# Four projections and half of the output product with 512 moving weight columns, and the retention's gate written in place

## The chip, the cores and the metric

The kernel runs on one core of a Trainium2 chip. A core has a matrix engine (TensorE, PE in the profile; its weight loads are a row of their own, PEld), VectorE (DVE), ScalarE (ACT), GpSimd (POOL) and SyncE (SP), which issues most of the DMAs that bring weights from HBM into SBUF. Each engine works off its own queue in order. The metric is the device time of one execution in microseconds; less is better.

## The reference, cut to what matters

The model is two transformer blocks on 256 tokens of width 1024, with 256 context tokens beside them. All of the change lies in the mixer and the merge of the first block.

```python
(gq, gk, gv, gg, glr_f, glr_b, rq, rk, rv, rg, m_gla, m_ret) = split_columns(h @ w_in)   # widths 512, 512, 1024, 1024, 16, 16, 512, 512, 1024, 1024, 1024, 1024
o_f, s_gf = gla_scan(gq, gk, gv, log_gate(glr_f, 0), states[0], False)
o_b, s_gb = gla_scan(flip(gq), flip(gk), flip(gv), flip(log_gate(glr_b, 1)), states[1], True)
o_gla = rmsnorm(o_f + flip(o_b), gla_norm) * jax.nn.silu(heads(gg, GLA_HEADS))
# rq and rk are turned by axial_rope for the latent tokens
r_f, s_rf = retention_scan(rq, rk, rv, lg_f, states[2], False)
r_b, s_rb = retention_scan(flip(rq), flip(rk), flip(rv), lg_b, states[3], True)
o_ret = head_groupnorm(r_f + flip(r_b)) * jax.nn.silu(heads(rg, RET_HEADS))
...
y = jax.nn.sigmoid(m_gla) * (o_gla @ w_branch_gla) + jax.nn.sigmoid(m_ret) * (o_ret @ w_branch_ret)
h_lat = h_lat + g1 * (y @ w_out)
```

gv, rv, gk and rk are needed for the latent and for the context tokens ("two streams"); gq, gg, rg and w_out for the latent tokens alone. A mixture of experts (MoE), a sparse attention block, a cross attention and an MLP follow.

## The kernel before, in words

**Precision.** Every product of activations and weights is made of three matmuls: activations and weights are each split into a high part in TensorE's reduced fp32 form and a remainder, and high×high, high×low and low×high are summed in PSUM. `split` (L285 to L287) does it for weights: a CAST on ACT makes `hi`, a TENSOR_TENSOR on DVE, or on POOL where the caller asks for it, makes `lo` = weight minus `hi`. A split covers 128x1024 numbers, half of a load of 1 MB. The pools of `hi` and `lo` have two buffers, the ring of loaded weights `wt` three; the rows of w_ada that DVE multiplies by the conditioning vector (L473) are loaded into the same ring.

**Projections.** `w_step` (L299 to L301) keeps the weights stationary and moves 256 tokens (tile `pw`); gq, gk, rq and rk use it. `x_step` (L312 to L314) keeps a tile of 128 tokens stationary and moves 256 weight columns (tile `px`). gv, rv, gg, rg and w_out use it in chunks of 256 columns, four for each matrix: 96 matmuls a chunk with two streams, 48 with one. A result of a chunk takes one PSUM bank (both token tiles beside each other). PSUM has six such banks, and two for transposes (`tp`).

**The stages around the change, in order of time.** `z` (the decay gate's products, to about 88 us); cumulative sums of the gate by DVE scans (L730: eight for the latent tokens, `sums(0)`, then eight for the context); gv and gq; the levels of GLA (`gla_levels`): for each of 16 level steps DVE makes four differences `E` (L782 to L785), ACT an exponential (L786), DVE a product with q and k (L787), and PE eight matmuls `lev` (L794); beside them run rk, rq (by `w_step`) and rv (by `x_step`), the retention's constants `crow` (L907, L908) and the rows of w_ada (L473 to L475). Then `gates("g")`: for each chunk of gg the ACT tanh and DVE product `sg` (L960, L961), the GLA output gated in place (`og`, L970) and `parts_chunk`, which transposes it (`tp`, L364) and splits it into `oTg` (L371). Beside it, pulled from a generator, runs `ret`: the rotation of rk and rq (`rot`, L857; DVE L858 to L861), the retention's scores (`rs`, L870) and its states and outputs (`or`, L887). `gates("r")` does the same for rg; the four results are copied by POOL into `srg` (L979), from which DVE gates the normed output `orr` (L987). After the merge with the two branch matrices comes w_out in four chunks: DVE multiplies by g1 (`otmp`, L1076) and adds to `h` (L1077), ACT sums squares (`junk`, L383), PE transposes `h` (`tp`, L1152), DVE and ACT scale it to `h2T` (L1154, L1156), and PE forms the router's logits (`rt`, L1163). The MoE's expert loads begin behind that.

**Order.** The program is written as generators that are pulled in a fixed order, and a layer of the kernel then orders the recorded instructions for each engine by dependences and costs. What stands in each engine's queue is therefore shown below from the built programs and not from the source.

In rv and rg, `lows=(PO, None)` gives the first half of every chunk's `lo` to POOL: eight instructions in all.

Of the kernel before, what the change touches and what calls it, by code (L numbers as in the profile page):

```python
# [14 lines left out]
ALU = mybir.AluOpType  # L15
# [15 lines left out]
def _chunks(w):  # L31

    k, n = w.shape
    return w.reshape(k // 128, 128, n // 256, 256).transpose(2, 1, 0, 3).reshape(n // 256, 128, -1)

# [65 lines left out]
def prepare(inp):  # L101
# [14 lines left out]
    out['w1'] = np.concatenate([_chunks(a) for a in (gk, gq, gv, rk, rq, rv, gg, rg, mg, mr)])  # L116
# [3 lines left out]
    out['w2'] = np.concatenate([_chunks(g[n][0]) for n in ('w_branch_gla', 'w_branch_ret', 'w_out')])  # L120
# [125 lines left out]
def pull(gen, n):  # L246
    for _ in range(n):
        if next(gen, 0) == 0:
            return


class Kern:
# [253 lines left out]
    def mixer(self, PA, PB, PC):  # L506
# [190 lines left out]
        def vproj(base, names, tags, done=None):  # L697
            a = tb([128, 2, D], tags[0], name=names[0])
            b = tb([128, 2, D], tags[1], name=names[1])
            st[names[0]], st[names[1]] = a, b  # L700
            for c in range(4):
                pc, pl = done if done and c == 0 else self.proj_x('w1', base + c, [SC, SL], lows=(None, None) if base == 4 else (PO, None))
                nc.scalar.copy(b[:, :, c * 256:(c + 1) * 256], pc.rearrange("p (t n) -> p t n", t=2))
                v.tensor_copy(a[:, :, c * 256:(c + 1) * 256], pl.rearrange("p (t n) -> p t n", t=2))
                yield
# [18 lines left out]
        pull(gv, 1)  # L724
# [224 lines left out]
        def gates(which, base, gain, hi, lo):  # L949
# [5 lines left out]
            for c in range(4):  # L955
# [11 lines left out]
        for c, sg, gn in gates("g", 16, None, hi, lo):  # L967
            cs = slice(c * 256, (c + 1) * 256)
            for i in range(2):
                v.scalar_tensor_tensor(og[:, i, cs], og[:, i, cs], st['rg'][:, 2 * c + i:2 * c + i + 1], sg[:, i], op0=ALU.mult, op1=ALU.mult)  # L970
            if c:
                self.parts_chunk(og, c - 1, gn, hi, lo)
        self.og_parts = (hi, lo)
        sgs = []
        srg = ta([128, 2, D], "B8", name="srg")
        for c, sg, _ in gates("r", 20, None, None, None):
            if c == 0:
                self.parts_chunk(og, 3, gn, hi, lo)
            nc.gpsimd.tensor_copy(srg[:, :, c * 256:(c + 1) * 256], sg)  # L979
# [40 lines left out]
    def merge(self, PB, PC):  # L1020
# [47 lines left out]
        for c in range(4):  # L1068
            po, = self.proj_x('w2', 8 + c, [(yh, yl)], wt=w2[c])
            last = self.last  # L1070
            if c < 2:
                w2.append(self.load_w('w2', 10 + c))
                more(2)
            cs = slice(c * 256, (c + 1) * 256)
            tmp = tb([128, 2, 256], "t3", name="otmp", bufs=1)
            v.tensor_tensor(tmp, po.rearrange("p (t n) -> p t n", t=2), g1[:, None, cs].to_broadcast([128, 2, 256]), op=ALU.mult)  # L1076
            v.tensor_tensor(h[:, :, cs], h[:, :, cs], tmp, op=ALU.add)  # L1077
            if c:
                turned(c - 1)
            if c > 1:  # L1080
                with self.tc.issue_after(last):
                    logits(c - 2)
# [1240 lines left out]
```

## Time and profile before

| | us |
|---|---|
| runs | 1072.5, 1072.56, 1068.6 (median 1072.5) |
| the profiled execution: its own time | 1070.49 |
| its span in the trace | 1068.7 |
| PE busy | 1012.1 (95%), 7182 matmuls |
| DVE busy | 641.9 (60%) |
| ACT busy | 449.1 (42%) |
| POOL busy | 74.8 (7%) |

The times of the parts come from the one profiled execution; 1.8 us of its 1070.49 lie outside the span. A busy PE is not PE at its peak, since matmuls overlap: what one costs in a stream is the distance from its start to the next one's start, which is shorter than its duration. Idle time of an engine is printed with the instruction that ended it.

### The profile page before, as it was taken

The page shows a single profiled execution, that of the slowest core. Times are in us where ns is not written, and L with a number is a line of the kernel's source. Part 1 is how long each engine was busy: PE and PEld are TensorE (multiplying, and loading weights), DVE is VectorE, ACT ScalarE, POOL GpSimd, SP SyncE. Part 2 cuts the span into 40 slices and gives each one's busy share as a digit, 9 for nine tenths or more (in the row PEclk, how much of TensorE's full clock was granted, in tenths as well). Part 3 has the DMA queues.
Part 4 walks back from the last instruction along what each step waited for, and adds up shares of the span by engine and source line. Part 5 has one row for each costly group of instructions (what it writes and reads, how often), then busy time and mean ns, then how long its engine had stood idle before and what let it go on. Part 6 is the DMA issues. An engine that isn't in the chain of part 4 may idle for free.

```text
span 1068.7 us, 17877 instructions
## 1 busy us (share of the span) xinstructions
PE 1012.1 (95%) x7182; PEld 819.1 (77%) x7182; DVE 641.9 (60%) x1195; ACT 449.1 (42%) x785; POOL 74.8 (7%) x69
## 2 busy tenths in 40 slices
PE   5999998999999999999999878898999999999998
PEld 3889998998989999944444412687756889999997
DVE  4467879896565465634424312789776647555554
ACT  4356444333334634422222101685465646444442
POOL 0200001200131000000000000122100000000000
PEclk9999999999999999999999999999989999999999
DMA  9822654773327887888999999943311425555552
GB/s 357 313 73 79 241 193 158 178 277 111 118 83 284 320 350 274 246 309 322 387 420 420 420 421 421 383 158 120 119 40 40 159 82 194 189 182 186 193 197 79
DMA packets 36197, 243.07 MB, mean 227 GB/s; under 512 B 4032, under 2 KB 4432, under 8 KB 8464
## 3 DMA queue, kind: packets, MB, share of 16 engines
q1 hardware_dynamic: 34800, 236.53, 59.2%
q0 software_dynamic: 1312, 5.37, 1.5%
q8 instruction: 57, 0.93, 0.3%
q14 instruction: 28, 0.23, 0.1%
HBM read 240.83 MB, written 1.06 MB: 226 GB/s over the span
## 4 chain that ended last, share of the span: by engine, by line
PE 33%; DMA 12%; DVE 5%; ACT 2%; POOL 1%; issue 1%; SPq 0%; DVEq 0%; POOLq 0%; ACTq 0%
DMA wt<-wgu_in 7%; DMA wt<-wdn_in 4%; PE pw L299 3%; PE pw L300 3%; PE pw L301 3%; PE gu L1484 3%; PE acc L2292 3%; PE acc L2291 3%; PE acc L2293 3%; PE dn L1515 2%; DVE lo L287 1%; PE sc L1534 1%; POOL rstd L355 1%; DMA nfin<-nfin_in 1%; PE pT L2087 1%
## 5 line engine op out<-in xcount | busy, mean ns | idle before, releaser
L287 DVE TENSOR_TENSOR lo<-wt,hi 128x1024 fp32r<-128x1024 f32 x171 | 209.8, 1229 | 123.6 <-ACT hi L285 123.3
L285 ACT CAST hi<-wt 128x1024 fp32r<-128x1024 f32 x180 | 188.1, 1047 | 197.9 <-PE pw L300 113.2
L1484 PE MATMUL gu<-wt,XT 128*32 128x512 f32 (+1 forms) x608 | 92.2, 607 | 9.0 <-DMA wt<-wgu_in 8.9
L301 PE MATMUL pw<-fh,lo 128*128 128x256 f32 x352 | 98.2, 280 | 2.1 <-DVE lo L287 2.1
L300 PE MATMUL pw<-fl,hi 128*128 128x256 f32 x352 | 98.8, 281 | 1.1 <-DVE fl L371 1.1
L299 PE MATMUL pw<-fh,hi 128*128 128x256 f32 x352 | 98.5, 280 | 0.0
L1484 PEld LDWEIGHTS gu<-wt,XT 128*32 128x32 f32 (+1 forms) x608 | 23.3, 115 | 63.0 <-issue 43.7
L313 PE MATMUL px<-lo,h0h 128*128 128x256 f32 x240 | 68.6, 286 | 2.1 <-DVE lo L287 1.5
L301 PE MATMUL pw<-h0h,lo 128*128 128x256 f32 x240 | 68.1, 284 | 2.2 <-DVE lo L287 2.2
L312 PE MATMUL px<-hi,h0h 128*128 128x256 f32 x240 | 68.9, 287 | 0.0
L301 PEld LDWEIGHTS pw<-fh,lo 128*128 128x128 f32 x352 | 66.9, 190 | 2.4 <-DVE lo L287 2.4
L299 PE MATMUL pw<-h0h,hi 128*128 128x256 f32 x240 | 68.5, 285 | 0.1
L300 PE MATMUL pw<-h0l,hi 128*128 128x256 f32 x240 | 67.9, 283 | 0.0
L314 PE MATMUL px<-hi,h0l 128*128 128x256 f32 x240 | 67.9, 283 | 0.0
L300 PEld LDWEIGHTS pw<-fl,hi 128*128 128x128 f32 x352 | 66.1, 188 | 2.0 <-DVE fl L371 1.5
L299 PEld LDWEIGHTS pw<-fh,hi 128*128 128x128 f32 x352 | 66.1, 188 | 0.6
L1515 PE MATMUL dn<-wt,hT 128*32 128x512 f32 (+1 forms) x320 | 55.8, 596 | 4.9 <-DMA wt<-wdn_in 3.4
L1492 DVE TENSOR_TENSOR hid<-hid,gu 128x256 f32<-128x256 f32 x12 | 5.1, 421 | 78.6 <-ACT hid L1491 78.6
L2292 PE MATMUL acc<-lo,rh 128*128 128x512 f32 x128 | 49.8, 389 | 0.0
L2291 PE MATMUL acc<-hi,rh 128*128 128x512 f32 x128 | 49.8, 389 | 0.0
L2293 PE MATMUL acc<-hi,rlo 128*128 128x512 f32 x128 | 49.8, 389 | 0.0
L313 PEld LDWEIGHTS px<-lo,h0h 128*128 128x128 f32 x240 | 46.0, 192 | 3.3 <-DVE lo L287 2.0
(643 smaller groups left out, 2518.9 us busy)
## 6 DMA issues: line engine op xcount, KB each, us to landing
wt<-wgu_in SPq DMA_DIRECT2D x60, 1024.0 KB, 16.6
wt<-w_in SPq DMA_DIRECT2D x48, 1024.0 KB, 5.0
wt<-wdn_in SPq DMA_DIRECT2D x31, 1024.0 KB, 19.4
wt<-wada_in SPq DMA_DIRECT2D x16, 1024.0 KB, 5.3
wt<-wfi_in SPq DMA_DIRECT2D x16, 1024.0 KB, 4.8
wt<-wfo_in SPq DMA_DIRECT2D x16, 1024.0 KB, 4.8
wada<-wada_in SPq DMA_DIRECT2D x8, 1024.0 KB, 9.8
wt<-wxkv_in SPq DMA_DIRECT2D x4, 1024.0 KB, 6.4
```

The costliest lines, as they stand in the source:

```text
L285: nc.scalar.copy(hi, src)
L287: self.low = (engine or nc.vector).tensor_tensor(lo, src, hi.bitcast(F32), op=ALU.subtract).ins
L299: nc.tensor.matmul(o, lhsT=hi[:, c], rhs=xh[:, x, :], start=k == 0 and b == 0, stop=False)
L300: nc.tensor.matmul(o, lhsT=hi[:, c], rhs=xl[:, x, :], start=False, stop=False)
L301: nc.tensor.matmul(o, lhsT=lo[:, c], rhs=xh[:, x, :], start=False, stop=k == 7 and b == 1)
L312: nc.tensor.matmul(o, lhsT=xh[:, k, s], rhs=hi[:, c], start=k == 0 and t == 0, stop=False)
L313: nc.tensor.matmul(o, lhsT=xh[:, k, s], rhs=lo[:, c], start=False, stop=False)
L1484: return lambda: nc.tensor.matmul(pg[a:a + n, :], lhsT=XT[:, k, c:c + n], rhs=w[:, kk * 512:(kk + 1) * 512], start=k == 0, stop=k == 7)
L1515: return lambda: nc.tensor.matmul(pd[nh][a:a + m, :], lhsT=hT[:, kk, a:a + m], rhs=w[:, kk * 1024 + nh * 512:kk * 1024 + (nh + 1) * 512], ...
L2291: nc.tensor.matmul(a, lhsT=rh[:, k, s], rhs=whi[:, w], start=c == 0 and k == 0, stop=False)
L2292: nc.tensor.matmul(a, lhsT=rh[:, k, s], rhs=wlo[:, w], start=False, stop=False)
L2293: nc.tensor.matmul(a, lhsT=rlo[:, k, s], rhs=whi[:, w], start=False, stop=last)
```

## The change

A new layout `_wide` puts 512 columns of eight k-tiles into two loads of 1 MB, each with four k-tiles; a new function `proj_xw` works on it: a split covers two k-tiles of 512 columns, and each matmul moves 512 columns into a PSUM bank for each token tile. It is used for the second half of gv, for all of rv, gg and rg, and for the first half of w_out: 1056 matmuls of 256 columns become 528 of 512. As many splits are made as before, of the same size. `proj_xw` has no choice of engine for `lo`: the eight on POOL are DVE's. A pair of chunks now has one point (half of the loads) at which other work is pulled in, and at its end two banks, one for each token tile, where two chunks had two ends. `gates` makes `sg` for each token tile (128x512), and for rg DVE writes it into `srg` directly, so that the four POOL copies go. gq's two chunks are moved ahead of the second half of gv. In the output product the first two chunks are one pair, and the transposes of both follow chunk 2.

```diff
+def _wide(w):
+    n = w.shape[1]
+    return w.reshape(2, 4, 128, n // 512, 512).transpose(3, 0, 2, 1, 4).reshape(n // 256, 128, -1)
...
+    def proj_xw(self, name, i, streams, outs, wts=None):
+        nc = self.nc
+        outs += [[self.bank("px") for _ in range(2)] for _ in streams]
+        for half in range(2):
+            wt = wts[half] if wts else self.load_w(name, i + half)
+            for q in range(2):
+                hi, lo = self.split(wt[:, q * 1024:(q + 1) * 1024])
+                for kk in range(2):
+                    k = 4 * half + 2 * q + kk
+                    c = slice(kk * 512, kk * 512 + 512)
+                    for (xh, xl), banks in zip(streams, outs):
+                        for t, o in enumerate(banks):
+                            s = slice(t * 128, t * 128 + 128)
+                            nc.tensor.matmul(o, lhsT=xh[:, k, s], rhs=hi[:, c], start=k == 0, stop=False)
+                            nc.tensor.matmul(o, lhsT=xh[:, k, s], rhs=lo[:, c], start=False, stop=False)
+                            self.last = nc.tensor.matmul(o, lhsT=xl[:, k, s], rhs=hi[:, c], start=False, stop=k == 7).ins
+            yield half
...
         pull(gv, 1)
+
+        def gq(c):
+            pl, = self.proj_w('w1', 2 + c, [SL])
+            return nc.scalar.mul(QK[:, 2 * c:2 * c + 2, 0, :], pl.rearrange("p (h t) -> p h t", h=2), 128.0 ** -0.5).ins
...
-        pull(gv, 1)
+        gq(0)
         for r in range(2):
             nc.scalar.activation(xx[r][:, :, 1:257], xx[r][:, :, 1:257], AF.Ln, bias=one)
...
+        late = gq(1)
         sums(0)
-        for c in range(2):
-            pl, = self.proj_w('w1', 2 + c, [SL])
-            late = nc.scalar.mul(QK[:, 2 * c:2 * c + 2, 0, :], pl.rearrange("p (h t) -> p h t", h=2), 128.0 ** -0.5).ins
...
-            for c in range(4):
-                pl, = self.proj_x('w1', base + c, [SL], lows=(None, None) if which == 'g' else (PO, None))
-                pv = pl.rearrange("p (t n) -> p t n", t=2)
-                pull(bg, 2 if which == "g" else 3)
-                sg = tb([128, 2, 256], "t2", name="sg", bufs=2)
-                nc.scalar.activation(sg, pv, AF.Tanh, scale=0.5)
-                v.scalar_tensor_tensor(sg, sg, 1.0, pv, op0=ALU.add, op1=ALU.mult)
-                yield c, sg, gn
+            for c in (0, 2):
+                outs = []
+                for half in self.proj_xw('w1', base + c, [SL], outs):
+                    for f in between if c + half == 0 else ():
+                        f()
+                    pull(bg, 2 if which == "g" else 3)
+                for t, pv in enumerate(outs[0]):
+                    sg = tb([128, 512], "t2", name="sg", bufs=2)
+                    nc.scalar.activation(sg, pv, AF.Tanh, scale=0.5)
+                    to = sg if into is None else into[:, t, c * 256:c * 256 + 512]
+                    v.scalar_tensor_tensor(to, sg, 1.0, pv, op0=ALU.add, op1=ALU.mult)
+                    yield c, t, sg, gn
...
-            nc.gpsimd.tensor_copy(srg[:, :, c * 256:(c + 1) * 256], sg)
...
+        for half in self.proj_xw('w2', 8, [(yh, yl)], pair, wts=w2):
+            w2.append(self.load_w('w2', 10 + half))
+            more(2)
+        for t in range(2):
+            added(pair[0][t], t, slice(0, 512))
+        for c in range(2, 4):
             po, = self.proj_x('w2', 8 + c, [(yh, yl)], wt=w2[c])
...
+            if c == 2:
+                turned(0)
+            turned(c - 1)
+            with self.tc.issue_after(last):
+                logits(c - 2)
```

The order in the queues changes at three places. DVE, from the latent tokens' scans to the context's, before (E are a level's differences and products, `lo` a weight remainder, `gvl` a copy of a finished gv chunk):

```order
L730 SCALAR_TENSOR_TENSOR xcl<-mn,xcl 128x256 x3
L782 TENSOR_TENSOR E<-xcl 128x2x128
...
L287 TENSOR_TENSOR lo<-wt,hi 128x1024
L784 TENSOR_TENSOR E<-xcl 128x2x2x64
L785 TENSOR_TENSOR E<-xcl 128x2x2x64
L730 SCALAR_TENSOR_TENSOR xcc<-mn,xcc 128x256 x8
L742 TENSOR_SCALAR sfb<-xcc 128x4
L704 COPY gvl<-px 128x2x256
L287 TENSOR_TENSOR lo<-wt,hi 128x1024 x3
L787 TENSOR_TENSOR E<-E,QK 128x1024 x2
```

and after the change:

```order
L295 TENSOR_TENSOR lo<-wt,hi 128x1024
L827 TENSOR_TENSOR E<-E,QK 128x1024
L824 TENSOR_TENSOR E<-xcl 128x2x2x64
L295 TENSOR_TENSOR lo<-wt,hi 128x1024
L825 TENSOR_TENSOR E<-xcl 128x2x2x64
L773 SCALAR_TENSOR_TENSOR xcc<-mn,xcc 128x256 x4
L827 TENSOR_TENSOR E<-E,QK 128x1024
L773 SCALAR_TENSOR_TENSOR xcc<-mn,xcc 128x256 x4
L947 TENSOR_SCALAR ctr<-ctr 128x512 x2
L948 TENSOR_TENSOR crow<-ctr,crow 128x512 x2
L295 TENSOR_TENSOR lo<-wt,hi 128x1024
```

The last `lo` here is that of the second quarter of gv's wide pair. The context's scans, one product E and the four `crow` instructions stand between it and the `lo` before it; the `crow` instructions stood behind two more groups of `lo` before.

PE, from the rotation of rq to the retention's first scores, before (`tp` transposes a gated chunk, `px` is the projection of gg):

```order
L857 MATMUL rot<-rQ,rc 128x512 x2
L364 MATMUL tp<-smalls,og 128x128 x4
L313 MATMUL px<-lo,h0h 128x256
L314 MATMUL px<-hi,h0l 128x256
...
L870 MATMUL rs<-rQ,rK 128x256 x4
L312 MATMUL px<-hi,h0h 128x256
L870 MATMUL rs<-rQ,rK 128x256 x4
```

and after the change:

```order
L897 MATMUL rot<-rQ,rc 128x512 x2
L392 MATMUL tp<-smalls,og 128x128
L910 MATMUL rs<-rQ,rK 128x256 x4
L373 MATMUL px<-hi,h0h 128x512
```

The 23 `px` matmuls that stood between the transposes and the scores stand behind the scores now. DVE's queue at the same place, after the change:

```order
L1005 SCALAR_TENSOR_TENSOR sg<-sg,px 128x512 x2
L898 TENSOR_TENSOR rt<-rot,rc 128x512 x2
L900 TENSOR_TENSOR rQ<-rQ,rc 128x1024
L1014 SCALAR_TENSOR_TENSOR og<-og,rstd,sg 128x256
L901 TENSOR_TENSOR rQ<-rQ,rt 128x1024
L1014 SCALAR_TENSOR_TENSOR og<-og,rstd,sg 128x256 x3
```

Both products `sg` of the finished gg pair stand ahead of the rotation's four instructions; `og` of the lone transpose stands between its last two.

PE, at the end of chunk 2 of w_out, before:

```order
L314 MATMUL px<-hi,yl 128x256
L1152 MATMUL tp<-smalls,h 128x128 x4
L1163 MATMUL rt<-mconst,h2T 128x36 x4
L312 MATMUL px<-hi,yh 128x256
L1152 MATMUL tp<-smalls,h 128x128 x4
L313 MATMUL px<-lo,yh 128x256
```

and after the change:

```order
L322 MATMUL px<-hi,yl 128x256
L1202 MATMUL tp<-smalls,h 128x128 x6
L1213 MATMUL rt<-mconst,h2T 128x36 x2
L1202 MATMUL tp<-smalls,h 128x128 x2
L1213 MATMUL rt<-mconst,h2T 128x36 x2
L1202 MATMUL tp<-smalls,h 128x128 x4
L320 MATMUL px<-hi,yh 128x256
L321 MATMUL px<-lo,yh 128x256
```

Twelve transposes and four logit products stand ahead of chunk 3's first `px`, in place of four and four.

## Rows read from the trace of the kernel before

**Rows 1.** The page's busy times (share, instructions), then, in tenths over 40 slices, clock and DMA.
```profile
PE 1012.1 (95%) x7182; PEld 819.1 (77%) x7182; DVE 641.9 (60%) x1195; ACT 449.1 (42%) x785; POOL 74.8 (7%) x69
...
PEclk9999999999999999999999999999989999999999
DMA  9822654773327887888999999943311425555552
```
**Rows 2.** Stretches: window, its length, busy PE PEld DVE ACT POOL, PEclk, DMA.
```profile
160.00:180.00 20.00, 17.25 (x143) 16.76 (x142) 19.82 (x31) 8.86 (x11) 3.27 (x1) 1.00 0.45 158
203.60:240.00 36.40, 36.40 (x279) 35.44 (x279) 35.85 (x56) 13.06 (x20) 3.56 (x2) 1.00 0.70 259
55.00:335.00 280.00, 270.04 (x2068) 258.25 (x2067) 215.07 (x340) 120.36 (x168) 34.40 (x24) 1.00 0.47 161
```
**Rows 3.** PE's waits from 55 to 335 us: releaser, us in total, times, longest.
```profile
PE lev L794 <- DVE E L787: 2.7, 2, 1.8
PE pw L301 <- DVE lo L287: 2.2, 1, 2.2
PE px L313 <- DVE lo L287: 1.5, 2, 1.3
PE rs L870 <- DVE rQ L861: 0.9, 1, 0.9
PE px L313 <- POOL lo L287: 0.7, 1, 0.7
```
**Rows 4.** Timeline of PE (start, duration): a chunk of rv; the attention's output product.
```profile
192.27 0.29 PE L314 MATMUL px<-hi,h1l 128*128 128x256 f32 x1
202.95 0.28 PE L313 MATMUL px<-lo,h0h 128*128 128x256 f32 x1
...
834.66 0.39 PE L1664 MATMUL acc<-lo,fh 128*128 128x512 f32 x1
837.18 0.39 PE L1663 MATMUL acc<-hi,fh 128*128 128x512 f32 x1
```
**Rows 5.** Timelines of POOL and DVE around POOL's first `lo` of rv.
```profile
173.26 3.27 POOL L287 TENSOR_TENSOR lo<-wt,hi 128x1024 fp32r<-128x1024 f32 x1 [117.31 <-ACT hi L285]
174.23 3.38 DVE L787 TENSOR_TENSOR E<-E,QK 128x1024 f32<-128x1024 f32 x1
181.97 1.21 DVE L787 TENSOR_TENSOR E<-E,QK 128x1024 f32<-128x1024 f32 x1
```
**Rows 6.** The page's sixth part, DMA issues: count, size, median us from issue to landing.
```profile
wt<-wada_in SPq DMA_DIRECT2D x16, 1024.0 KB, 5.3
```
**Rows 7.** Timeline of DVE in the gv stage.
```profile
95.85 4.76 DVE L730 TENSOR_TENSOR_SCAN xcc<-mn,xcc 128x256 f32<-128x256 f32 x8
101.18 2.35 DVE L287 TENSOR_TENSOR lo<-wt,hi 128x1024 fp32r<-128x1024 f32 x2
113.24 0.42 DVE L907 TENSOR_SCALAR ctr<-ctr 128x512 f32<-128x512 f32 x1
113.70 0.69 DVE L908 TENSOR_TENSOR crow<-ctr,crow 128x512 f32<-128x512 f32 x1
```
**Rows 8.** Timeline of DVE around the rotation of rq.
```profile
258.32 1.28 DVE L858 TENSOR_TENSOR rt<-rot,rc 128x512 f32<-128x512 f32 x2
262.18 0.68 DVE L961 SCALAR_TENSOR_TENSOR sg<-sg,px 128x512 f32<-128x512 f32 x1
264.16 0.48 DVE L970 SCALAR_TENSOR_TENSOR og<-og,rstd,sg 128x256 f32<-128x256 f32 x1
```
**Rows 9.** Timelines of DVE and ACT around the end of w_out's chunk 2.
```profile
435.55 0.69 DVE L1076 TENSOR_TENSOR otmp<-px,g 128x512 f32<-128x512 f32 x1 [3.37 <-PE px L314]
436.54 0.68 DVE L1077 TENSOR_TENSOR h<-h,otmp 128x512 f32<-128x512 f32 x1
...
436.13 1.04 ACT L285 CAST hi<-wt 128x1024 fp32r<-128x1024 f32 x1
437.32 0.42 ACT L383 ACTIVATE junk<-h 128x256 f32<-128x256 f32 x1
```

More of the change, by code (lines that the diff above doesn't have):

```diff
@@ L115, in prepare @@
     gq, gk, gv, gg, lf, lb, rq, rk, rv, rg, mg, mr = [w[:, o[i]:o[i + 1]] for i in range(12)]
-    out['w1'] = np.concatenate([_chunks(a) for a in (gk, gq, gv, rk, rq, rv, gg, rg, mg, mr)])
+    out['w1'] = np.concatenate([_chunks(a) for a in (gk, gq, gv[:, :512])] + [_wide(gv[:, 512:])] + [_chunks(a) for a in (rk, rq)]
+                               + [_wide(a) for a in (rv, gg, rg)] + [_chunks(a) for a in (mg, mr)])
     same = np.tile(np.eye(32, dtype=np.float32), (4, 4))
     out['wlr'] = np.concatenate([np.concatenate([lf, lb], 1).reshape(8, 128, 32).transpose(1, 0, 2).reshape(128, -1), same], 1)
-    out['w2'] = np.concatenate([_chunks(g[n][0]) for n in ('w_branch_gla', 'w_branch_ret', 'w_out')])
+    wo = g['w_out'][0]
+    out['w2'] = np.concatenate([_chunks(g[n][0]) for n in ('w_branch_gla', 'w_branch_ret')] + [_wide(wo[:, :512]), _chunks(wo[:, 512:])])
     lw = np.zeros((4, 2, 16, 2, 512), np.float32)
@@ L700, in vproj @@
             st[names[0]], st[names[1]] = a, b
-            for c in range(4):
-                pc, pl = done if done and c == 0 else self.proj_x('w1', base + c, [SC, SL], lows=(None, None) if base == 4 else (PO, None))
-                nc.scalar.copy(b[:, :, c * 256:(c + 1) * 256], pc.rearrange("p (t n) -> p t n", t=2))
-                v.tensor_copy(a[:, :, c * 256:(c + 1) * 256], pl.rearrange("p (t n) -> p t n", t=2))
+            if done:
+                for c in range(2):
+                    pc, pl = self.proj_x('w1', base + c, [SC, SL]) if c else done
+                    nc.scalar.copy(b[:, :, c * 256:(c + 1) * 256], pc.rearrange("p (t n) -> p t n", t=2))
+                    v.tensor_copy(a[:, :, c * 256:(c + 1) * 256], pl.rearrange("p (t n) -> p t n", t=2))
+                    yield
+            for c in range(2 if done else 0, 4, 2):
+                outs = []
+                for half in self.proj_xw('w1', base + c, [SC, SL], outs):
+                    if half == 0:
+                        yield
+                for t in range(2):
+                    nc.scalar.copy(b[:, t, c * 256:c * 256 + 512], outs[0][t])
+                    v.tensor_copy(a[:, t, c * 256:c * 256 + 512], outs[1][t])
                 yield
@@ L947, in mixer, with gates @@
         bg = ret()
-        def gates(which, base, gain, hi, lo):
+        def gates(which, base, into=None, between=()):
             gn = None
@@ L954, in gates @@
                                 0.5, None, op0=ALU.mult)
-            for c in range(4):
-                pl, = self.proj_x('w1', base + c, [SL], lows=(None, None) if which == 'g' else (PO, None))
-                pv = pl.rearrange("p (t n) -> p t n", t=2)
-                pull(bg, 2 if which == "g" else 3)
-                sg = tb([128, 2, 256], "t2", name="sg", bufs=2)
-                nc.scalar.activation(sg, pv, AF.Tanh, scale=0.5)
-                v.scalar_tensor_tensor(sg, sg, 1.0, pv, op0=ALU.add, op1=ALU.mult)
-                yield c, sg, gn
+            for c in (0, 2):
+                outs = []
+                for half in self.proj_xw('w1', base + c, [SL], outs):
[8 more added lines that the diff above has]
+                    yield c, t, sg, gn
@@ L965, in mixer @@
         hi, lo = (tb([128, 8, 256], "h1" + n, F32R, name="oTg") for n in "hl")
         og = st['og']
[L967 to L972, printed above, removed]
+        for c, t, sg, gn in gates("g", 16):
+            for d in range(2):
+                cs = slice((c + d) * 256, (c + d + 1) * 256)
+                v.scalar_tensor_tensor(og[:, t, cs], og[:, t, cs], st['rg'][:, 2 * (c + d) + t:2 * (c + d) + t + 1],
+                                       sg[:, d * 256:(d + 1) * 256], op0=ALU.mult, op1=ALU.mult)
+            if c and t:
+                for d in range(2):
+                    self.parts_chunk(og, d, gn, hi, lo)
@@ L973, in mixer @@
         self.og_parts = (hi, lo)
-        sgs = []
         srg = ta([128, 2, D], "B8", name="srg")
-        for c, sg, _ in gates("r", 20, None, None, None):
-            if c == 0:
-                self.parts_chunk(og, 3, gn, hi, lo)
-            nc.gpsimd.tensor_copy(srg[:, :, c * 256:(c + 1) * 256], sg)
+        for _ in gates("r", 20, srg, [lambda c=c: self.parts_chunk(og, c, gn, hi, lo) for c in (2, 3)]):
+            pass
         pull(bg, 99)
@@ L1067, in merge, with added @@
         more(2)
-        for c in range(4):
+        def added(po, t, cs):
+            tmp = tb([128, 2, 256], "t3", name="otmp", bufs=1)
+            tmp = tmp if t is None else tmp.rearrange("p t n -> p (t n)")
+            t = slice(None) if t is None else t
+            v.tensor_tensor(tmp, po, g1[:, cs] if isinstance(t, int) else g1[:, None, cs].to_broadcast([128, 2, 256]), op=ALU.mult)
+            v.tensor_tensor(h[:, t, cs], h[:, t, cs], tmp, op=ALU.add)
+        pair = []
+        for half in self.proj_xw('w2', 8, [(yh, yl)], pair, wts=w2):
+            w2.append(self.load_w('w2', 10 + half))
+            more(2)
+        for t in range(2):
+            added(pair[0][t], t, slice(0, 512))
+        for c in range(2, 4):
             po, = self.proj_x('w2', 8 + c, [(yh, yl)], wt=w2[c])
             last = self.last
[L1071 to L1082, printed above, removed]
+            added(po.rearrange("p (t n) -> p t n", t=2), None, slice(c * 256, (c + 1) * 256))
+            if c == 2:
[3 more added lines that the diff above has]
+                logits(c - 2)
         self.ahead[4:4] = w0
```

## The prediction

> **What bounds the kernel now.** I read first the busy shares of the page: the matrix engine is busy for 95% of the span, every other compute engine for 60% or less [rows 1]. So a microsecond comes either out of the matmuls themselves or out of the few places where PE waits. Then the clock and the DMA row over the 40 slices [rows 1]: the clock is at full speed (2.4 GHz) except in one slice, so no gain is to be had there; the DMA engines are full only in the slices of the MoE (21 to 25 of 40). The mixer lies before them, and the expert loads are issued behind the output product, so that I take what the mixer saves or loses to move all that follows. Then the stretches [rows 2]: from 55 to 335 us, where all of the change but the output product lies, PE is busy for 270.04 of 280 us. In rv (203.6 to 240) PE is busy for all 36.40 us, though DVE is too for 35.85; from 160 to 180 DVE is busy for 19.82 of 20 us and PE for only 17.25: there DVE sets the pace. Last the waits [rows 3]: 2.7 us for DVE's level product, 2.2 for one `lo` in the gq chunk, 1.5 and 0.7 for `lo` in rg, 0.9 for the rotated rq. They say what there is to win besides the matmuls: about 8 us, of which 4.9 hang on POOL's part (the first, third and fifth row).
>
> All sums are made against the profiled execution's own 1070.49 us, 2.0 below the median of the three runs shown (1072.5) and within their spread. About 0.5% (5.4 us) is what a measurement of this kernel can tell from no change.
>
> **The change part by part.**
>
> *Wider matmuls.* In the stream of rv, 89 steps lie between the two 256-column rows shown, 10.68 us: 0.120 us each. In the attention's output product, which has the same three-matmul form with 512 columns, 11 steps take 2.52 us: 0.229 each [rows 4]. Two of 256 cost 0.240, one of 512 costs 0.229, so 0.011 us is saved 528 times: **-5.8 us**, on the path, since PE is the bound wherever these run. The weight loads fall by 528 too; they overlap the matmuls in both forms. The bounds are 0 (the mixer's stream gains nothing) and -5.8.
>
> The Trainium skill ("TensorE: Matmul & The Clock Gate", Back-to-back issue gap) gives an isolated gap of N/2.4 + 2.5 ns at the warm clock. By it a pair of 256 would cost 218.4 ns and one of 512 215.8: 2.5 ns a pair, an estimate of 1.3 us in all in place of 5.8. The rows disagree with it on both forms (120 and 229 ns).
>
> *POOL's eight `lo`.* While POOL works on one, for 3.27 us, DVE's product that started beside it takes 3.38 us; the same product undisturbed takes 1.21 [rows 5]. DVE is held until POOL is done, so each POOL `lo` takes about 2.2 us from DVE, where doing it itself costs 1.2. Six of the eight stand so in the trace. Moving them to DVE therefore costs 8 x 1.2 = 9.8 us there and gives back about 6 x 2.2 = 13: DVE's load falls by some 3 us, and it falls where DVE is the bound. The waits behind it (2.7, 1.5 and 0.7 us [rows 3]) go: -4.9 us at most. Something is late next, however: after the change a product with a row of w_ada (L501) stands in DVE's queue ahead of a `lo` and level products, and its load can be issued only when the ring slot of rq's last half is free; such a load takes 5.3 us to land [rows 6]. Laid against the queue, it comes about 2 us late. I give back 1.5 of the 4.9, between 0 (the load is early) and 4.9 (everything returns as another wait): **-3.4 us**. The four `srg` copies on POOL were waited for by DVE alone; they go at no gain or loss to PE.
>
> *gq ahead of gv's wide pair.* Before, two chunks of gv (192 matmuls, 23 us of PE work) ran beside the eight latent scans, and PE waited for none of the `lo` among them [rows 3]. Now one chunk runs, then gq at once. (a) The second half of gq's first `lo` stands behind five scans of 0.6 us: about 1.8 us of PE idle. (b) gq's second chunk: 0.6. (c) The `lo` of gv's second quarter stands behind eight scans (4.76 us), one product E (1.2), and two pairs of `ctr` and `crow` (2 x 1.1) [rows 5, 7]: with a difference E, 8.5 us after the `lo` ahead of it. PE has one quarter, 24 matmuls of 0.229 or 5.5 us, to do meanwhile: about 3.1 us idle. (d) Behind the two copies `gvl` the first `lo` of rk comes 0.9 us late, and one quarter 0.2. Together 6.6; the 2.2 of before [rows 3], which was the same cause at another place (eight context scans ahead of two `lo`), goes: **+4.4 us**. Bounds: 0, if DVE reaches these instructions earlier than I lay them, and +6.6.
>
> *The gates.* The 23 matmuls of gg that covered the rotation of rq stand behind the scores now. From the end of the first gg pair DVE does two `sg` (0.68 each, the first after ACT's tanh), two `rt` (1.28 both), one product with the cosine (1.2, as the 128x1024 product in rows 5), one `og` (0.48), and the sum (1.2) [rows 5, 8]: 5.5 us, or 5.0 with the overlap of one instruction into the next. PE has the rotation and a lone transpose, about 1 us. So `rs` waits 4 us where it waited 0.9 [rows 3]: **+3.0 us**, with bounds of 0 (DVE is early: one of the two `sg` is done while the pair's last matmuls run) and +4.
>
> *The output product.* Its 48 wide matmuls are in the first term. At the end of chunk 2, PE has twelve transposes and four logit products ahead of chunk 3, of which the last four need the sum `h` of chunk 2 (`otmp` and `h`, 0.7 us each, with an `h2T` between them [rows 9]); before, four transposes and four logit products stood there, and chunk 3 had begun. ACT's `hi` for chunk 3 falls behind four `junk` (0.6 each with its readout) in place of two [rows 9]. I take **+1.2 us**, between 0 and 2.4 (all four `junk` in the way).
>
> Sum: -5.8 - 3.4 + 4.4 + 3.0 + 1.2 = -0.6, **1069.9 us, say 1070: no difference that can be told.**
>
> **The rivals.**
>
> *The orders cost nothing.* If DVE is ahead of PE at the two new places, because what I count behind each other is done while PE still streams, the width and POOL's part count whole: -5.8 - 4.9, with +1 for the tail, -9.7: 1060.8. For it speaks that PE waits so little in this stretch now (10 of 280 us [rows 2]) and that DVE is idle for 65 of them. Against it, that `lo` waits on scans already once [rows 3], for 2.2 us, and that the queues have the `lo` further behind.
>
> *The banks.* A wide pair with two streams holds four of the six PSUM banks from its first matmul until both copies are made; a chunk held two. If DVE's copies are late, the next pair, which touches four banks within its first twelve matmuls, has to wait, and `lev` has only two banks beside it. DVE's backlog in rv (35.85 of 36.40 us busy [rows 2]) says that a copy may stand behind three or four products of 1.2 us, some 4 us, at the two ends of rv's pairs: +8 on top of the sum, 1078: **slower**. It decides from the point where the backlog exceeds the `lev` group and the work in the banks that are free, about 2 us. Against it: in rv's queue as I read it the copies stand near the front, and PE never waits there now.
>
> *The width gives nothing.* If what makes 256 columns take 0.120 us in the mixer grows with the columns there, one of 512 takes 0.240, and 0 stands in place of 5.8: 1075.7. The attention's rows, of the same form, take 0.229 [rows 4], which speaks against it. By the gap in the Trainium skill's section named above it would be 1074.4, with 1.3 in place of 5.8.
>
> **How the numbers follow.** My sum 0.50; the orders cost nothing 0.26; the banks 0.18; no gain from width 0.06. The likeliest is my sum: 1070. The range: the first rival lies at 1060.8 and the second at 1078; half of the first and a little more than half of the second are taken in, and the ends of the sum's own bounds in the gv stage and the gates (about 6.5 us down, 4.5 up) lie within: 1063 to 1077. Faster by over 0.5% means below 1065.1: the first rival and a corner of my sum, 0.27. Slower by over 0.5% means above 1075.9: the banks and a corner of the sum, 0.19. Within: 0.54.
>
> **What would show it.** The width: steps of 0.229 in gv, rv, gg, rg, and PE's count lower by 528. POOL: no `lo` before the MoE, no DVE product of over 2 us in 170 to 215. gv: PE waits on `lo` of gq and of gv's second quarter, together some 6 us; if they sum to under 3, my largest loss is wrong and the time is nearer 1064. Gates: a wait of `rs` on rQ of 3 to 4 us. Banks: a wait of `px` or `lev` on a copy would show that rival. A slice of the granted clock below full speed in the mixer would make all of it wrong.

## The result: slower by half a percent

The changed kernel takes 1077.65 us by the median of seven runs (1071.82 to 1081.35), the kernel before 1070.75 in the same comparison (1068.6 to 1072.56). The ratio is 1.0056, with a 95% interval of 1.0036 to 1.0076. I had forecast no difference, 1070 us in a range up to 1077: the time lies above the range, and it moved the other way than my sum (-0.6).

The profiled execution of the changed kernel took 1079.73 us. Its page, the counterpart of the first line of [rows 1] (busy us, share of the span, instructions), and its clock row, which stands in tenths over 40 slices:

```profile
PE 1012.3 (94%) x6654; PEld 797.2 (74%) x6654; DVE 639.0 (59%) x1203; ACT 449.1 (42%) x785; POOL 48.9 (5%) x57
...
PEclk9999999999999999999999999999989999999999
```

PE has 528 instructions fewer and is busy for as long as before. The clock row is that of before [rows 1], with its one 8 in the 30th slice, far behind the mixer. In the mixer it shows nothing, because a slice is 27 us long and a dip of a few us leaves it above 0.9; but the mean granted clock of the run is 0.988, and it was 0.995 before. Among the seven runs, the only one with a mean clock of 0.995 took 1071.82 us; the six with 0.984 to 0.990 took 1076.1 to 1081.4.

PE's waits from 55 to 340 us in the changed kernel, to be laid beside [rows 3] (releaser, us in total, times, longest):

```profile
PE px L374 <- DVE lo L295: 4.1, 3, 2.4
PE lev L834 <- DVE E L827: 3.5, 2, 3.4
PE pw L309 <- DVE lo L295: 2.7, 3, 1.7
PE tp L392 <- DVE og L1014: 2.4, 1, 2.4
PE rs L910 <- DVE rQ L901: 0.9, 1, 0.9
```

Beside them two small waits (z, 1.5 us in two rows, and ktp, transposes of k, 0.4) are the same in both kernels. Without those, PE waits 13.6 us where it waited 8.0. Three waits are long: 2.45 us in gv's wide pair, 3.37 at a level, and 2.42 and 0.90 one behind the other in the gates. Cut out the stretch of each wait and the one behind it, and the clock shows up (window, length, PE busy, granted clock, DMA share, GB/s):

```profile
108.70:111.10 2.40, 0.03 (x1) 0.99 0.00 0
111.10:114.50 3.40, 3.33 (x8) 0.50 0.71 217
...
183.60:186.20 2.60, 0.01 (x1) 0.99 0.96 400
186.20:193.00 6.80, 6.02 (x18) 0.50 0.48 164
...
268.00:271.60 3.60, 0.52 (x2) 0.99 0.00 0
271.60:275.00 3.40, 3.16 (x9) 0.51 0.00 0
```

After each of the three, PE has work again and does it at 1.2 GHz, for 3.4, 6.8 and 3.4 us. The timeline of PE behind the middle one (start, duration) shows what that is worth:

```profile
186.98 2.04 PE L834 MATMUL lev<-E 128*128 128x128 f32 x8 [3.37 <-DVE E L827]
...
191.38 0.63 PE L373 MATMUL px<-hi,h0h 128*128 128x512 f32 x1
191.81 0.63 PE L374 MATMUL px<-lo,h0h 128*128 128x512 f32 x1
...
193.05 0.39 PE L374 MATMUL px<-lo,h0h 128*128 128x512 f32 x1
...
201.47 0.40 PE L375 MATMUL px<-hi,h0l 128*128 128x512 f32 x1
```

At the low clock the 512-column matmuls start 0.43 us apart; behind it, 37 steps from 193.05 to 201.47 take 8.42 us, 0.228 each. So 0.47 of the time that PE works in a low stretch is lost: of 3.33 + 6.02 + 3.16 = 12.5 us, 5.9. (The rest of the stretches is wait, counted there: the middle one begins 0.8 us before its wait ends.) The Trainium skill ("TensorE: Matmul & The Clock Gate", HAM oscillation — how this bites in real kernels) says that a wait for operands can send the engine back to its lower clock, so that the work behind the wait starts slow; the three pairs of rows agree.

**Where the 9.2 us between the two profiles lie.** The start of the first z product is 2.1 us later (72.31 against 70.20) in code that the change does not touch; there the clock was low from 22.2 us on for 3.4 us in the changed kernel's profile, and so it was in most of the profiles below. From the last z to the first matmul of the output product, the stretch of the change, it took 351.2 us in place of 344.5: +6.7. From rows: waits +5.6, low clock +5.9, width -0.0124 x 480 = -6.0 (worked out below), in all +5.5; 1.2 us stay unexplained. The output product takes 26.71 us from its first px to the last, in place of 26.48. Outside this stretch both profiles hold as much low clock: 3.4 us from 637.7 and 6.8 from 781.0 on before, 3.4 from 22.3 and 6.8 from 790.3 on after the change.

### The profile page after: what moved, and what is told of

Read it like the earlier page. It is cut to its first block, busy times and chain, and to the rows that moved or that the text cites. A ratio compares the mean times of both kernels' runs of the same rounds, so it can differ in the third digit from the quotient of the medians.

```text
span 1078.0 us, 16802 instructions
## 1 busy us (share of the span) xinstructions
PE 1012.3 (94%) x6654; PEld 797.2 (74%) x6654; DVE 639.0 (59%) x1203; ACT 449.1 (42%) x785; POOL 48.9 (5%) x57
## 4 chain that ended last, share of the span: by engine, by line
PE 34%; DMA 11%; DVE 5%; ACT 2%; POOL 1%; issue 1%; SPq 0%; DVEq 0%; POOLq 0%; ACTq 0%
DMA wt<-wgu_in 7%; DMA wt<-wdn_in 4%; PE pw L308 3%; PE pw L307 3%; PE pw L309 3%; PE gu L1534 3%; PE acc L2342 3%; PE acc L2341 3%; PE acc L2343 3%; PE dn L1565 2%; PE sc L1584 1%; PE gat L1492 1%; POOL rstd L383 1%; DVE lo L295 1%; PE pT L2137 1%; PE sc L2107 1%
## 5 line engine op out<-in xcount | busy, mean ns | idle before, releaser
L295 DVE TENSOR_TENSOR lo<-wt,hi 128x1024 fp32r<-128x1024 f32 x179 | 219.4, 1227 | 134.0 <-ACT hi L293 134.0
L309 PEld LDWEIGHTS pw<-h0h,lo 128*128 128x128 f32 x240 | 46.3, 193 | 2.7 <-DVE lo L295 2.7
L307 PEld LDWEIGHTS pw<-h0h,hi 128*128 128x128 f32 x240 | 46.2, 193 | 0.3 <-ACT h0h L644 0.2
L308 PEld LDWEIGHTS pw<-h0l,hi 128*128 128x128 f32 x240 | 46.3, 193 | 0.0
L374 PE MATMUL px<-lo,h0h 128*128 128x512 f32 x112 | 44.6, 398 | 1.5 <-DVE lo L295 1.5
```

The costliest lines, as they stand in the source:

```text
L295: self.low = (engine or nc.vector).tensor_tensor(lo, src, hi.bitcast(F32), op=ALU.subtract).ins
L307: nc.tensor.matmul(o, lhsT=hi[:, c], rhs=xh[:, x, :], start=k == 0 and b == 0, stop=False)
L308: nc.tensor.matmul(o, lhsT=hi[:, c], rhs=xl[:, x, :], start=False, stop=False)
L309: nc.tensor.matmul(o, lhsT=lo[:, c], rhs=xh[:, x, :], start=False, stop=k == 7 and b == 1)
L374: nc.tensor.matmul(o, lhsT=xh[:, k, s], rhs=lo[:, c], start=False, stop=False)
```

## Experiments

Two theories. **Theory 1, the clock:** the waits cost more than their length, since PE works slowly behind the long ones. **Theory 2:** the low stretches come by chance or cost nothing, and the loss is the waits alone (or the wide matmuls gain less than the rows say). Nine kernels ran; ratios are to the kernel before, run beside them.

| kernel | median us (runs) | ratio, 95% interval |
|---|---|---|
| changed kernel again | 1078.22 (6) | 1.0061, 1.0037 to 1.0085 |
| idle matmuls in its waits | 1074.52 (12) | 1.0031, 1.0014 to 1.0049 |
| before, with waits added | 1089.65 (4) | 1.0165, 1.0139 to 1.0192 |
| three reorderings | 1065.90 (6) | 0.9944, 0.9924 to 0.9964 |
| before, POOL part alone | 1071.25 (12) | 0.9987, 0.9969 to 1.0004 |
| four reorderings | 1060.29 (6) | 0.9899, 0.9876 to 0.9922 |
| three reorderings, old output product | 1065.46 (10) | 0.9939, 0.9915 to 0.9964 |
| w_ada reordering alone | 1073.68 (12) | 1.0015, 0.9998 to 1.0033 |
| four reorderings, old output product | 1062.22 (6) | 0.9913, 0.9886 to 0.9940 |

### The changed kernel again

No edit.

> The changed kernel once more, for its waits and its clock on this chip. Theory 1 (the clock): its 7 us over the sum that I had worked out come from stretches at 1.2 GHz that begin when PE's three long waits end (2.45 us in gv's wide pair, 3.37 at a level, 2.42 and 0.90 in the gates): the same three stretches again, 1076 to 1080 us. Theory 2 (chance): the clock falls at other places or not at all, and the time stays 1076 to 1080 whatever it does.

Measured: 1078.22 us. The waits are the same to 0.3 us (2.47, 3.70, 2.42 and 0.90), and so are the places of the low clock (same columns as above):

```profile
110.80:114.20 3.40, 3.40 (x9) 0.52 0.68 222
186.20:192.80 6.60, 6.03 (x18) 0.50 0.49 161
271.50:274.70 3.20, 3.00 (x7) 0.50 0.00 0
```

That chance put three stretches at the same three places twice is unlikely; theory 2 is left with "they cost nothing".

### Idle matmuls in the waits

Three calls of a new function add matmuls whose result nothing reads; the first, in gv's wide pair, is made with `fill` = 9; `lm` is the last matmul of the level before, `rm` the last of the rotation.

```diff
+    def fill(self, n, after=None):
+        ps = self.bank("fil", "tp")
+        xh = self.SL[0]
+        x = xh[:, 0:2, :].rearrange("p a b -> p (a b)")
+        with self.tc.issue_after(after) if after else nullcontext():
+            for _ in range(n):
+                i = self.nc.tensor.matmul(ps, lhsT=xh[:, 0, 0:128], rhs=x, start=True, stop=True).ins
...
+                if fill and half == 0 and q == 1:
+                    self.fill(fill, self.last)
...
+                    if hp == 1 and w == 32:
+                        self.fill(13, lm)
...
+                if u is rQ:
+                    self.fill(12, rm)
```

> The changed kernel with 34 matmuls of 512 columns added, whose results nothing reads: 9 (2.1 us) behind the first quarter of gv's wide pair, 13 (3.0 us) ahead of the level group that waited 3.37 us, 12 (2.7 us) behind the rotation of rq. What PE waited for comes no earlier; PE only works meanwhile. Theory 1: no stretch at 1.2 GHz at these three places, and the time falls by 5 to 7 us against the changed kernel, to about 1071, though more is computed. Theory 2: the same time as the changed kernel or up to 2 us more, 1077 to 1080.

Measured: 1074.52 us, 3.7 below the changed kernel, with a wide spread (1069.31 to 1079.21). In its profiled run (1071.53) the three places are at full clock (same columns):

```profile
108.40:110.94 2.54, 1.18 (x6) 1.00 0.00 0
110.94:114.40 3.46, 3.46 (x15) 1.00 0.69 215
...
186.20:193.00 6.80, 6.80 (x32) 1.00 0.86 308
...
267.80:272.00 4.20, 4.20 (x19) 1.00 0.17 23
```

From the last z to the output product it took 345.9 us where the changed kernel took 351.2, though 34 matmuls, 7.8 us of work by the rows' 0.228, were added, and the waits that are left and the added work together are longer than the waits were. That decides against theory 2 for this run: useless work in the waits made the stretch 5.3 us shorter. The median falls by 3.7 only, less than the 5 to 7 that theory 1 expected. The other runs' mean clocks go down to 0.990, and where they fell was not traced; waits of 1.71, 1.47 and 1.36 us were left in this kernel, and the order of some level work on DVE shifted as well, so that the split between clock and order is not clean here.

### The kernel before, with waits added

```diff
-            self.low = (engine or nc.vector).tensor_tensor(lo, src, hi.bitcast(F32), op=ALU.subtract).ins
+            for _ in range(1 + self.again):
+                self.low = (engine or nc.vector).tensor_tensor(lo, src, hi.bitcast(F32), op=ALU.subtract).ins
+            self.again = 0
...
+            self.again = (2, 3, 4, 0)[c]
             pr, = self.proj_w('w2', 4 + c, [self.or_parts])
```

> The kernel before, with the `lo` of the first half of a weight chunk worked out three, four and five times instead of once at three places of the merge (w_branch_ret's chunks 0, 1 and 2), where PE never waits now: a `lo` takes 1.15 us and PE has some 0.5 us in hand, so that PE waits about 1.8, 2.9 and 4.1 us there, 8.8 in all. Theory 1: after the longer two the clock falls to 1.2 GHz and the time rises by 8.8 plus 1.7 to 3.4 for each fall, by 12 to 15 us. Theory 2: the clock stays and the time rises by 8.8, or less where later work takes some of it back.

Measured: 1089.65 us, 18.4 more than the median of before beside it: above both. The waits came out longer than I had laid them, since a product of the merge slipped in among the repeated `lo`. PE's three waits, and the stretches behind the longer two:

```profile
381.96 0.38 PE L305 MATMUL pw<-oTr,lo 128*128 128x256 f32 x1 [2.15 <-DVE lo L290]
398.21 0.42 PE L305 MATMUL pw<-oTr,lo 128*128 128x256 f32 x1 [4.47 <-DVE lo L290]
417.20 0.58 PE L305 MATMUL pw<-oTr,lo 128*128 128x256 f32 x1 [5.73 <-DVE lo L290]
```

```profile
376.00:392.00 16.00, 13.85 (x115) 1.00 0.74 275
392.00:398.40 6.40, 1.93 (x16) 1.00 0.99 404
398.40:401.80 3.40, 3.40 (x17) 0.50 1.00 371
...
408.00:415.40 7.40, 3.47 (x29) 1.00 0.44 144
415.40:422.20 6.80, 5.00 (x23) 0.51 0.45 154
```

The waits sum to 12.35 us. In the low stretches at the last two PE works for 3.4 and 5.0 us (the second begins 1.8 us before its wait ends), and for 3.4 us in one at 104.8, behind a wait of 2.22 that the kernel before has as well. In them matmuls of 256 columns start 0.213 us apart (15 steps from 398.43 to 401.63), in place of 0.120, so that 0.44 of the 11.8 us is lost, 5.2: 17.5 with the waits. The stretch from the last z to the output product took 362.9 us in place of 344.5 in the profile of before: 18.4 more. With the waits as they were, theory 2 gives 12.35. So a kernel with none of the change's wide matmuls falls in the same way: a wait is enough for it, without the width. The wait of 2.15 us was not followed by a fall, the one of 2.22 was.

### Three reorderings

gq's chunks go back behind the first half of gv's wide pair; the w_ada rows of the second rq chunk are pulled one step later; in the gates the scores `rs` are pulled one step later.

```diff
-        gq(0)
+        pull(gv, 1)
         for r in range(2):
             nc.scalar.activation(xx[r][:, :, 1:257], xx[r][:, :, 1:257], AF.Ln, bias=one)
...
-        late = gq(1)
         sums(0)
+        gq(0)
+        late = gq(1)
...
             pull(lev, 2)
-            pull(ada12, 1)
+            pull(ada12, 1 - c)
-        for _ in vproj(12, ("rvl", "rvc"), ("R1", "M1")):
+        for n, _ in enumerate(vproj(12, ("rvl", "rvc"), ("R1", "M1"))):
             pull(lev, 2)
-            pull(ada12, 1)
+            pull(ada12, 2 if n == 0 else 1)
...
-                    pull(bg, 2 if which == "g" else 3)
+                    pull(bg, (2, 1, 2, 2)[c + half] if which == "g" else 3)
```

> The changed kernel with three places put in another order, all of its wide matmuls kept: gq's chunks stand where they stood before (behind the first half of gv's wide pair), the w_ada rows of the second rq chunk are worked on one step later, and the retention's scores are pulled one step later, so that projection matmuls lie between the rotation of rq and its scores. The three long waits should be gone or under 1 us. Theory 1: no stretch at 1.2 GHz in the mixer, the waits' 8 us and the clock's 6.8 us come back: about 1062 to 1065. Theory 2: the waits' 8 us alone: about 1069 to 1071.

Measured: 1065.90 us, 12.3 below the changed kernel beside it and faster than the kernel before, ratio 0.9944. Waits from 55 to 340 us and the one low stretch that is left in the mixer:

```profile
PE pw L309 <- DVE lo L295: 2.2, 1, 2.2
PE lev L835 <- DVE E L828: 2.0, 2, 1.1
PE px L374 <- DVE lo L295: 1.4, 1, 1.4
PE rs L911 <- DVE rQ L902: 0.2, 1, 0.2
```

```profile
101.30:103.60 2.30, 0.06 (x2) 1.00 0.00 0
103.60:104.20 0.60, 0.60 (x5) 1.00 0.00 0
104.20:107.60 3.40, 3.40 (x19) 0.51 0.88 292
```

The waits (without z and ktp) are 5.8 us, 7.8 less than in the changed kernel; the low clock costs 0.44 x 3.4 = 1.5 in place of 5.9, 4.4 less. Together 12.2, against 12.3 by the medians and 13.3 from the last z to the output product (337.9 in place of 351.2). Theory 2 has 7.8 of it. "No stretch at 1.2 GHz in the mixer" did not come: one is left, behind a wait of 2.24 us.

### The POOL part alone, on the kernel before

In rv as shown, and in rg in the same way:

```diff
-                pc, pl = done if done and c == 0 else self.proj_x('w1', base + c, [SC, SL], lows=(None, None) if base == 4 else (PO, None))
+                pc, pl = done if done and c == 0 else self.proj_x('w1', base + c, [SC, SL], lows=(None, None))
...
-                v.scalar_tensor_tensor(sg, sg, 1.0, pv, op0=ALU.add, op1=ALU.mult)
+                to = sg if into is None else into[:, :, c * 256:(c + 1) * 256]
+                v.scalar_tensor_tensor(to, sg, 1.0, pv, op0=ALU.add, op1=ALU.mult)
...
-            nc.gpsimd.tensor_copy(srg[:, :, c * 256:(c + 1) * 256], sg)
```

> The kernel before with the POOL part of the change alone: all eight `lo` on DVE, srg written in place, no wide matmul, no other order. My prediction's term: PE's waits of 2.7 (levels), 1.5 and 0.7 us (`lo` in rg) go, so -3 to -5 us: 1066 to 1068. Rival: DVE's stretched instructions were off PE's path or come back as later waits: 1070 to 1072, the kernel before's time.

Measured: 1071.25 us, ratio 0.9987: by the time, the rival is right, no difference. In the trace the waits did fall, by some half of the 4.9 us that the prediction's rows gave:

```profile
PE pw L301 <- DVE lo L287: 2.2, 1, 2.2
PE px L313 <- DVE lo L287: 1.3, 1, 1.3
PE lev L794 <- DVE E L787: 0.9, 1, 0.9
PE rs L870 <- DVE rQ L861: 0.9, 1, 0.9
```

They are 2.6 us less than in [rows 3] (5.4 against 8.0), and the stretch from the last z to the output product takes 343.1 us in place of 344.5, with a low stretch behind the 2.2 us wait (3.3 us from 105.06 at a clock of 0.52) that the profile of before does not have and that takes back 1.5. Four of its twelve runs took 1064.9 to 1068.3 and eight 1070.8 to 1073.2. So POOL's part is worth 2.6 us of PE's waits, and no difference that these runs could tell.

### Four reorderings

As the three, and the context's scans are held behind the last `lo` of gq:

```diff
         late = gq(1)
+        low = self.low
...
-        sums(1)
+        with tc.issue_after(low):
+            sums(1)
```

> The kernel with the three places reordered, and the context's eight scans put behind the last `lo` of gq, for which PE still waits 2.24 us with 3.4 us at 1.2 GHz behind it. Theory 1 (the clock): that wait and the low stretch both go, -2.2 and -1.7: about 1062. Theory 2 (waits only): -2.2: about 1063.7. If the scans' later place makes a level or ktp late: the same 1066.

Measured: 1060.29 us, ratio 0.9899: faster than both kernels, by 1.0% against before. It is 5.6 below the three reorderings by the medians (of two sittings), more than the 3.9 that theory 1 expected. The traces show less: from the last z to the output product 335.2 us in place of 337.9, that is 2.7, since the wait of 2.2 us went with its low stretch, but a level waits 0.5 us longer and a `lo` of rk is waited for:

```profile
PE pw L309 <- DVE lo L295: 0.5, 1, 0.5
```

The clock in the mixer is at 1.00 (window, length, busy PE, PEld, DVE, ACT, POOL, clock, DMA share, GB/s):

```profile
55.00:335.00 280.00, 273.35 (x1666) 242.40 (x1666) 216.45 (x355) 125.91 (x176) 8.25 (x11) 1.00 0.51 167
429.30:432.70 3.40, 3.40 (x18) 3.40 (x17) 1.23 (x2) 0.56 (x3) 0.00 (x0) 0.52 0.70 246
```

Its profiled run is the slowest of its six (1064.68), and the last row shows a part of why: the clock fell in the output product, where the longest wait is 0.88 us, and for 6.8 us more from 439.5 on.

### The old output product, with three and with four reorderings

The four chunks of before take the place of the pair and the grouped transposes; w_out's layout goes back too.

```diff
-        for half in self.proj_xw('w2', 8, [(yh, yl)], pair, wts=w2):
...
+        for c in range(4):
+            po, = self.proj_x('w2', 8 + c, [(yh, yl)], wt=w2[c])
...
+            if c:
+                turned(c - 1)
```

> The kernel with the three places reordered, and the output product as it was before the change (four chunks of 256 columns, their transposes one chunk apart). My prediction's terms: the twelve transposes at the end of chunk 2 cost 1.2 us, the 48 wide matmuls save 0.5: so -0.7, 1065.2. Rival: the output product's new order costs nothing, +0.5: 1066.4. Either is inside what can be told by the time, so the length of the stage, from the router bias (rtb) to the last px, is read in the trace: 26.5 us or more with the wide pair, 26.5 without it.

> The four reorderings together with the output product as it was before the change. In the profile of the kernel with the four reorderings alone, stretches at 1.2 GHz lie at 429.3 (3.4 us) and 439.5 (6.8 us), beside the output product's transposes, where PE waits 0.35 and 0.88 us. Theory 1 (the clock): with the shorter waits of the old order (0.41 and 0.42 us) they are gone, and the stage from the first px to the last takes 26.5 us in place of 28.2: 1058 to 1060 by the median of runs. Theory 2: the clock falls there by chance, in some runs of either, and the time is the same 1060 to 1061.

Measured: 1065.46 and 1062.22 us, the same as with the wide pair (1065.90 and 1060.29) as far as the intervals tell. From the first px to the last, the stage takes 26.45 us with the old order and 26.71 with the wide pair, at full clock; the price of the grouped transposes and the gain of width nearly cancel. With four reorderings the old order takes 26.46, where the wide pair with its low stretch took 28.22; but right behind it, among the router's logits, the clock fell in the old order too (440.6 to 444.0), and the medians do not differ. The three reorderings' profile has the wide pair's waits too (0.35 and 0.88 us), and no fall. So theory 2 holds here: a fall in this stage is not tied to the wide pair's longer waits.

### The w_ada reordering alone

The changed kernel with the second of the three edits.

> The changed kernel with only the w_ada rows of the second rq chunk worked on one step later. The level's wait of 3.4 to 3.7 us should go, and what is left are the waits in gv and in the gates. Theory 1 (the clock): the stretch of 6.8 us at 1.2 GHz goes with it, the other two stay: -3.5 - 3.4, about 1071 to 1072. Theory 2 (waits only): about 1074.5 to 1075.

Measured: 1073.68 us, 4.5 below the changed kernel (medians of two sittings), between the two theories. The level's wait is gone (0.38 us) and the low stretch of 6.8 us with it. But the one behind the gates' waits of 2.42 and 0.90, 3.4 us in the changed kernel, is 6.8 us here:

```profile
262.00:265.20 3.20, 0.61 (x2) 0.98 0.00 0
265.20:272.00 6.80, 6.08 (x15) 0.51 0.18 36
```

In the stretch from the last z to the output product it saves 4.5 us: 3.1 of wait and 0.47 x 3.0 = 1.4 of clock (PE works for 9.5 us at the low clock, in place of 12.5). Two of its twelve runs have a mean clock of 0.997: they took 1067.4 and 1067.8.

## Why the prediction was wrong

**The step that failed first is how a wait was priced.** I read the clock row [rows 1], saw full speed in all but one slice, and wrote that "no gain is to be had there". That the change could lose there I left to one sentence at the end. Every wait in my sum cost its length. The three long ones cost 9.1 us of length and 5.9 us of low clock besides. With that term the sum of -0.6 is +5.3; measured were +6.9 by the medians. That the -0.6 itself fits the rest was luck: the terms as measured below (-6.5, 0, +3.1, +2.4, +0.8) come to -0.2, because 3.4 us too much for POOL stood against 3.0 that I had too dear in the other four.

The trace of the kernel before had the sign in it. The one slice that I passed over is the 30th (775 to 801 us): there PE waited 1.20 and 0.64 us for ACT, and from 781.0 on it worked at 1.2 GHz for 6.8 us. Another stretch lies in the 24th slice, whose digit is a 9 (same columns as above):

```profile
634.00:637.50 3.50, 1.04 (x2) 1.00 1.02 419
637.50:641.00 3.50, 3.17 (x16) 0.52 0.99 414
```

There PE had waited for expert weights, 1.34 and 1.45 us with one microsecond of work between, and then worked at half the clock; I take it that it cost little, because the DMA engines were full.

**Wider matmuls: right.** -5.8 was forecast with 0.0110 a pair from the attention's rows; in rv the pair is 0.240 - 0.228 = 0.0124 apart, 6.5 us in all. Against the POOL part alone, the three reorderings save 5.2 us from the last z to the output product (343.1 and 337.9, both with one low stretch, with 5.4 and 5.8 us of waits) for 480 of the 528 pairs; 5.3 was forecast for these, 6.0 goes by rv's step.

**POOL's `lo`: the mechanism right, the returned part mis-sized.** The step that failed is "I give back 1.5 of the 4.9". DVE waited for the w_ada load as I had said, but longer, and the level's product stood behind it:

```profile
183.33 1.22 DVE L501 SCALAR_TENSOR_TENSOR wt<-wt,crow 128x1024 f32<-128x1024 f32 x1 [2.91 <-DMA wt<-wada_in]
184.48 1.22 DVE L295 TENSOR_TENSOR lo<-wt,hi 128x1024 fp32r<-128x1024 f32 x1
185.62 1.22 DVE L827 TENSOR_TENSOR E<-E,QK 128x1024 f32<-128x1024 f32 x1
```

The level waits became 3.5 us where they were 2.7, the `lo` of rg 1.5 where it was 2.2: all of the 4.9 came back, so that the term is 0 and not -3.4. Alone, and with the w_ada row in its old place, the part takes 2.6 us out of the waits: the other 2.2 of the 4.9 stay even there.

**gq ahead of gv: right place, a little too much.** Forecast 6.6 us of waits, measured 1.71 + 0.42 + 2.45 + 0.18 + 0.57 = 5.3, which is +3.1 instead of +4.4. The one that decided is (c), the `lo` behind the scans and `crow`: 3.1 forecast, 2.45 found, and a low stretch behind it.

**The gates: right.** Forecast 4 us, measured 2.42 for the lone transpose and 0.90 for the scores, 3.3, which is +2.4 instead of +3.0. Most of the wait fell on the transpose, which waits for `og`, and not on the scores, where I had laid it.

**The output product: right within its bounds.** Forecast +1.2 beside a width gain of 0.5, that is +0.7; the stage grew by 0.2, so that the order cost some 0.8.

**The rivals.** "The orders cost nothing" had 1060.8, and the four reorderings take 1060.29; but these are other orders than the change's, and one of them takes away a wait of 2.2 us that the kernel before had, so that the near match is in part luck. The banks did not matter: no px or lev waited for a copy in rv in the changed kernel's profile. The last rival, no gain from width, is wrong by the 0.0124 us a pair.

**What stays open.** A wait of 2.2 us at the same place in the gv stage was followed by a low stretch in four profiles (the kernel before with waits added, POOL alone, three reorderings with either output product) and not in the profile of the kernel before; in the output product the clock fell after waits of less than 1 us in two of the profiles. How often each place falls in runs without a profile of their places is not known, so that single medians here may carry 2 to 4 us of it, an estimate from the two groups of runs of the POOL part alone. In the reordered kernels' profiles the falls outside the mixer are not all at the places where they were before, and the medians are not corrected for that. Of the +6.9, 1.2 us have no term.

## What to carry to other kernels

On a matrix-bound kernel, price a new wait of TensorE like those here (2.2 to 5.7 us) at its length and at the slow work that may follow it (5.9 us for three of them), and look for pairs of a nearly idle stretch and one at half the clock in the trace before you price anything: a row with 27 us in a slice hides them. A change that saves on each matmul can be lost to two or three new waits; here four reorderings of PE's and DVE's work turned +0.6% into -1.0% with the same matmuls. When an order is generated, read every engine's queue at the places where a producer now stands behind work that nobody waits for (scans, constants, rows whose load is late).

## What the runs showed of the hardware

- Filling waits with matmuls that nothing reads made the mixer faster in the traced run: 345.9 us in place of 351.2 with 34 matmuls more.
- The stretch behind the same wait is not always as long: 3.4 us at 1.2 GHz behind the gates in the changed kernel's profiles, 6.8 in the one with the w_ada edit.
- The Trainium skill's page on TensorE ("TensorE: Matmul & The Clock Gate", What's actually happening) puts the penalty of the clock's ramp, at the first matmuls of a kernel, at under 1% of a typical kernel's span. The falls in the midst of this kernel are another case, of the same size: 5.9 of 1078 us in the mixer, 0.5%, nearly as large as the whole result.
- The kernel before varies by its clock too: of 17 runs on one chip, the one with a mean clock of 0.997 took 1067.84 us, those with 0.990 took 1073.4 and 1075.3; but one with 0.993 took 1073.9, so that the clock is not all of it.
